# Moving the splits of two weight products in a two-layer MLP kernel: product 2's into a later matmul, product 7's ahead of product 4's

## The chip, the cores and the metric

The kernel runs on one core of one Trainium2 chip. The metric is device time in microseconds (us), the median of several runs. The engines are named as in the profile: PE (matmul) with PEld (its weight loads), DVE (vector), ACT (scalar), POOL (GpSimd) and SP, which here only issues transfers. Transfers are also issued by POOL; all of them are carried out by the DMA engines.

## The reference

```python
def reference(x, w1, w2):          # x 8x1024x1024, w1 1024x4096, w2 4096x1024, f32
    h = x @ w1
    h = 0.5 * h * (1 + np.tanh(np.sqrt(2 / np.pi) * (h + 0.044715 * h ** 3)))
    return (h @ w2).astype(np.float32)
```

## The kernel before

The 8192 rows of x are taken in eight superblocks of 1024 rows. In each, a first matmul makes g = gelu(x w1), and a second one makes g w2. Operands are f16, sums f32. Both matmuls are done by a Strassen scheme: a 2x2 block product takes seven products (numbered 1 to 7) of sums of blocks in place of eight. Products 1, 2 and 3 take plain blocks of the weights, products 4, 5, 6 and 7 take sums of blocks (`W1_SUM`, `W_SUM`). Where the operands of a product are split once more in the same manner, the product itself is seven smaller ones; the code calls these *inner* ones, and a product that is done so is *deep* here (`Inner`, line 1046; its matmuls are line 1118).

The first two superblocks also prepare data for the others. They keep in DRAM the blocks and sums of w1 and w2 (`w1_d`, `w2_d`) and, for each product m of the second matmul, four further sums of quarters of its weights, **the splits of m** (`in_d[m]`). Superblocks 3 to 8 do all seven products of the second matmul deep and load these splits.

- `matmul1` (line 533) is the first matmul of superblocks 1 and 2 (in the code `sb` 0 and 1). It runs over eight pairs j of columns; each pair is seven products of two halves h, with matmuls of 512 columns (line 499). For each pair of superblock 2 it also makes sums of w1 on DVE (`MadeQuad.sum`, `inner_sums`) and stores them from POOL. `half = 3 if j % 2 else 0` says how many of these jobs stand in the middle of a pair, with the rest at its end.
- `matmul2_made` (line 844) is the second matmul of superblocks 1 and 2. Its products run in the order 1, 2, 5, 6, 3, 7, 4, over four row groups q of 128 rows each; a row group is 16 matmuls of 512 columns (line 1160). One product is deep: product 3 in superblock 1, product 4 in superblock 2.
- `FILL[sb]` (line 46) is an order written by hand: after the matmuls of row group q (or deep step n) of product m, the jobs under `mq` are put into DVE's order. `w` makes a quarter of a sum of w2, `p` makes one split of a product (two DVE instructions of 128x1024) and stores it from POOL (512 KB), `a` makes an inner sum of g for the deep product, `g` sums of g, `x`, `q` and `i` sums of the next superblock's x and w1.
- `split_jobs` (line 995) makes a product's four splits: splits 7 and 4 into tiles of the pool `mp` (tile name `mu`, two buffers), splits 5 and 6 into common tiles (pool `up`, tile name `u`, 24 buffers). In superblock 2 product 7's splits all take common ones. The deep product's weights are its own splits (`deep.y = parts[deep.m]`), so their tiles are held until its steps have used them.
- `split_in_m1` (line 1012) can make splits in `matmul1` of superblock 2 from blocks that it loads back from `w2_d`; `SPLIT_IN_M1` (line 39) is empty, so it isn't used.
- `StoredHalf` (line 270) loads half a quad of w1 operands for superblocks 3 to 8: six groups of 512 KB, of which the group `("s1", "s5")` goes into a `mu` tile, the others into `u` tiles. From half 3 on that `mu` tile is filled by POOL (`make`, line 305). `MadeQuad(0, False, True)` loads the first w1 blocks of superblock 2.

Instructions that are pinned (`keep_in_program_order`) keep the program's order on their engine; other transfers are placed by the compiler's scheduler, but each queue carries them out in the order of its list. A tile can be written only when the last user of its buffer is done, and that includes the landing of a store from it. The row `SPq` in the profile is SP's queue.

Of the kernel before, what the change touches and what calls it, by code (L numbers as in the profile page):

```python
# [35 lines left out]
h40 m54 g121' e20 s0 z73 x37 z21 a1 d' e21 m73 m31 h61 q0 u0 m74 p1 g220  # L36
""".split()
BEGIN = {"m37": (0,), "m24": (1,2), "m34": (3, 4)}
SPLIT_IN_M1 = ()


def slots(table):
# [5 lines left out]
    ;20:g50 w50 w51;21:g51 w52;22:w53 g52;23:g53 p14  # L48
    ;50:w60 w61;51:w62 w63;52:g30 g31;53:g32 g33
    ;60:p35 p36;61:p37 a37;62:p34 a36;63:a35  # L50
    ;31:w70;32:a33;33:w71;34:w72;35:w73;36:p25;37:p26
    ;70:p27 p24;71:w40 w41;72:w42 w43;73:x5;40:x7 x6;41:x3 q5;42:q6 q7 q4
    ;43:i2 i7 i3 i1 i5""".replace("\n    ", "")),
    slots("""10:g60 w50;11:g61 w51;12:g62 w52;13:g63 w53
    ;20:g50 p55;21:g51 p56;22:g52 p57;23:g53 p54
    ;50:w60 w61;51:w62 w63;52:g30 g31;53:g32 g33
    ;60:p65 w70;61:p66 w71;62:p67 w72;63:p64 w73
    ;30:w40 w41;31:w42 w43;32:p45 x5;33:p46 x7
    ;70:p47 a47;71:p44 a46;72:a45 p75;73:p76
    ;41:a43;42:p77;43:p74;44:x6;45:x3;46:i2;47:i3""".replace("\n    ", "")),  # L60
)


# [11 lines left out]
def kernel(  # L75
# [457 lines left out]
    def matmul1(xs, sb, quads, start=None):  # L533
# [26 lines left out]
        for j in range(NI // 2):  # L560
            cs = (2 * j, 2 * j + 1)
            end = j == NI // 2 - 1
            source = quads[j // 2]
            if start is not None and j == 0:
                start.pair(gelu)
                ahead(j)
                continue
            jobs = list(ahead(j))
            banks_a = [psum(), psum()]
            a = [temp(), temp()]  # L570
            for h in range(2):
                product(banks_a[h], source, xs, 1, cs[h], True)
                act_copy(a[h], banks_a[h])
            banks_c, p5, t = [], [], [temp(), temp()]

            def five(h):
                if len(p5) == h:
                    banks_c.append(psum())
                    p5.append(temp())
                    product(banks_c[h], source, xs, 5, cs[h], True)  # L580
                    act_copy(p5[h], banks_c[h])

            def six(h):
                product(banks_a[h], source, xs, 6, cs[h], False)
                act_copy(t[h], banks_a[h])

            def seven(h):
                product(banks_a[h], source, xs, 7, cs[h], False)
                tt(p5[h], banks_a[h], p5[h], SUB, True)

            def three(h):
                product(banks_c[h], source, xs, 3, cs[h], False)

            banks_b = [psum(), psum()]
            for h in range(2):
                if late is not None:
                    gelu("12", late[1][h], late[3][h])
                if j == 0:
                    product(banks_b[h], source, xs, 2, cs[h], True)
                if late is not None:  # L600
                    product(late[2][h], late[0], xs, 4, late[1][h], False)
                    gelu("21", late[1][h], late[2][h])
                elif j == 0:
                    five(h)
            for h in range(2 if j else 0):
                product(banks_b[h], source, xs, 2, cs[h], True)
            for h in range(2):
                add(a[h], banks_b[h])
            difference(g, j - 1)
            half = (len(jobs) + 1) // 2  # L610
            if start is not None and j == 1:
                rest = jobs[2:]
                half, jobs = 2, [lambda m=m: quads[0].sum(m, (2, 2), True) for m in (7, 4)] + jobs[:2]
            elif start is not None and j == 2:
                half, jobs = 2, rest
            if sb == 1:
                half = 3 if j % 2 else 0
                if j != 4:
                    jobs += splits
                    splits = []  # L620
            for job in jobs[:half]:
                job()
            if end:
                six(0)
                gelu("11", cs[0], a[0])
                six(1)
                gelu("11", cs[1], a[1])
                for h in range(2):
                    five(h)
                for h in range(2):  # L630
                    seven(h)
                    gelu("22", cs[h], p5[h])
                    three(h)
                for h in range(2):
                    product(banks_a[h], source, xs, 4, cs[h], False)
                    gelu("21", cs[h], banks_a[h])
                for h in range(2):
                    tt(t[h], t[h], banks_c[h], SUB, True)
                    gelu("12", cs[h], t[h])
            else:  # L640
                first = j == 0
                five(0)
                if not first:
                    gelu("11", cs[0], a[0])
                five(1)
                six(0)
                if not first:
                    gelu("11", cs[1], a[1])
                six(1)
                for h in range(2 if first else 0):  # L650
                    gelu("11", cs[h], a[h])
                three(0)
                three(1)
                seven(0)
                seven(1)
                for h in range(2):
                    gelu("22", cs[h], p5[h])
                for h in range(2):
                    tt(t[h], t[h], banks_c[h], SUB, True)
                late = (source, cs, banks_a, t)  # L660
            for job in jobs[half:]:
                job()
            if sb == 1 and j < 2 * len(SPLIT_IN_M1):
                splits = split_in_m1(SPLIT_IN_M1[j // 2], j % 2)
            if sb == 1 and j > 4:
                for q in {5: (0,), 6: (1,), 7: (2, 3)}[j]:
                    nxt["xb"] = x_cast_paced(sb + 1, g["11"][:, 2 * j + 1, :], 2 * q, nxt.get("xb"))
# [176 lines left out]
    def matmul2_made(sb, g, keep_w1, xb):  # L844
# [44 lines left out]
        def rows(t, q):  # L889
# [3 lines left out]
        operands = {1: "11", 2: "12", 4: "22", 7: "21", 5: "11", 3: "12"}  # L893
        parts = {m: {} for m in (1, 2, 3, *SUMS)}
        splits = {
            m: split_jobs(m, lambda m=m: pieces(m), parts[m], () if sb and m == 7 else (7, 4)) for m in parts
        }
        deep = Inner((3, 4)[sb], g[("12", "22")[sb]])
        deep.y = parts[deep.m]

        def run(key):
            for job in FILL[sb].get(key, ()):
# [6 lines left out]
                elif kind == "g":  # L909
                    tt(rows(g["12"], n), rows(g["12"], n), s2[n], SUB, True)  # L910
                elif kind == "w":
                    make(m, n)
                elif kind == "p":
                    splits[m][SUMS.index(n)]()
                elif kind == "a":
                    deep.make(n)
                elif kind == "x":
                    xs.make(m, pin=True)
                elif kind == "q":
                    quad.sum(m, pin=True)  # L920
                elif kind == "i" and sb:
                    xs.make_inner(m)
                elif kind == "i":
                    quad.inner_sums(m)

        into = []
        before_deep = {3: 6, 4: 7}[deep.m]

        def post(m, q, bank):
            if m == before_deep:  # L930
                if q % 2 == 0:
                    into.append(half())
                so_far = into[q // 2][:, q % 2, :]
            if m == before_deep == 6:
                tt(so_far, p5[q], bank, ADD, True)
            elif m in (1, 5, 6):
                t = {1: a, 5: p5, 6: t6}[m]
# [6 lines left out]
            else:  # L944
                t = {2: a, 3: t6, 7: p5}[m][q]
                tt(t, t, bank, ADD, True)
                at[q] = store(sb, {2: "11", 3: "12", 7: "22"}[m], q, t)
            if m == before_deep == 7:
                act_copy(so_far, bank)

        bring("11", pool_copy, False)
# [6 lines left out]
        for m, name, first in (  # L958
            (1, "a", True), (2, "b", True), (5, "c", True), (6, "a", False),
            (3, "c", False), (7, "a", False), (4, "a", False),  # L960
        ):
            if m == deep.m:
                deep.pieces = pieces(m)
                deep.base = into
                deep.rows = lambda r, t: store_rows(sb, {3: "12", 4: "21"}[m], r, t)
                for n in deep.steps(into):
                    if n == 7 and sb == 0:
                        quad = MadeQuad(0, False, True)
                    if n == 1 and sb:
                        quad = StoredHalf(0)  # L970
                    run((m, n))
                continue
            for q in range(NQ):
# [8 lines left out]
                    xs = XOps(x_transpose(xb, load_in_order))  # L982
                if (m, q) == (6, 0):
                    keep("22")
                if (m, q) == (1, NQ - 1) and sb == 0:
                    sums[5] = [unit(2, HALF) for _ in range(NI // QC)]
                    for t in sums[5]:
# [4 lines left out]
                run((m, q))  # L992
        return xs, [quad]

    def split_jobs(m, pieces, t, narrow=(7, 4)):

        def operand(v, h):
            if isinstance(v, int):
# [3 lines left out]

        def make(n):
            u, op, v = W_SUM[n]
            t[n] = (mp.tile([P, NI // 2, OH // 2], DT, name="mu") if n in narrow else unit(NI // 2, OH // 2))
            for h in range(2):
                tt(t[n][:, h * QC:(h + 1) * QC, :], operand(u, h), operand(v, h), op, True)
            nc.gpsimd.dma_start(out=in_d[m][:, SUMS.index(n)], in_=t[n])
# [3 lines left out]
    def split_in_m1(m, h):  # L1012
# [7 lines left out]
        def make(i, n):  # L1020
            u, op, v = W_SUM[n]
            if i % 2 == 0:
                t["two"] = gcp.tile([P, 2, HALF], DT, name="gc")
            t[n] = t["two"][:, i % 2]
            in0, in1 = (
                t[b] if isinstance(b, int) else raw[int(b[0]) - 1][:, int(b[1]) - 1] for b in (u, v)
# [272 lines left out]
```

## Time and profile before

| | |
|---|---|
| median of three runs | 1464.2 us (1462.4, 1464.2, 1464.36) |
| the profiled execution | 1462.14 us |
| its span, first to last instruction | 1460.4 us |
| PE busy / DVE busy / ACT busy / POOL busy | 99% / 84% / 46% / 42% |
| granted TensorE clock | 0.999 |
| second superblock, first matmul | 207.9 to 306.8 us |
| second superblock, second matmul | 306.8 to 401.9 us (product 3 from 362.0, product 7 from 375.9, deep product 4 from 389.6) |
| bytes moved by DMA | 472.73 MB, 324 GB/s over the span |

A line of a timeline gives the start and the length of a group of neighbouring instructions, engine, line, operation, `out<-in` by tile names, the count, and in brackets how long the engine stood idle before and what ended that. A line of waits gives who waited for whom: the sum in us, how often, and the longest. A line of the windows gives, for a stretch of time, each engine's busy us, then the granted clock, the busy share of the DMA engines and the GB/s that they moved.

### The profile page before, as it was taken

Reading aid. Unit: us, or ns where it says so; the run is one execution under the profiler, and the core shown is the slowest. Engines: PE = TensorE matmul, PEld = TensorE weight load, DVE = VectorE, ACT = ScalarE, POOL = GpSimd, SP = SyncE. Lnnn points to the kernel's source line nnn. Section 1 sums busy time; section 2 is a strip of 40 time slices with the busy share of each in tenths; the row PEclk is TensorE's granted clock in tenths of the full one; section 3 lists DMA queues with packets and bytes.
Section 4 is the critical chain, followed back from the end, with each engine's and each line's share of the span. In section 5 each row is a group of like instructions: output and inputs, shape, how many; then the busy total and the mean of one; then the engine's idle time right before and its main releaser. Section 6 shows DMA issues by size and latency. Waiting matters only on the chain.

```text
span 1460.4 us, 28936 instructions
## 1 busy us (share of the span) xinstructions
PE 1446.1 (99%) x10731; PEld 1046.6 (72%) x10731; DVE 1230.3 (84%) x2053; ACT 678.8 (46%) x1402; POOL 620.2 (42%) x630
## 2 busy tenths in 40 slices
PE   8999999999999999999999999999999999999998
PEld 4444644444567888778877788777887778877887
DVE  5657878657888999889998899988998889988887
ACT  5665016631068511784128831388215872068510
POOL 1542222212359411792138821498105961168311
PEclk9999999999999999999999999999999999999999
DMA  9999999797899999999999999999999999996597
GB/s 314 353 349 382 323 319 362 277 281 252 296 353 278 296 351 357 388 254 340 333 382 357 243 373 333 386 322 240 398 335 371 310 263 376 357 386 220 215 370 251
DMA packets 205646, 472.73 MB, mean 324 GB/s; under 512 B 75584, under 2 KB 80704, under 8 KB 204608
## 3 DMA queue, kind: packets, MB, share of 16 engines
q1 hardware_dynamic: 177632, 373.35, 73.8%
q0 software_dynamic: 27872, 97.53, 22.3%
q8 instruction: 84, 1.38, 0.4%
q14 instruction: 58, 0.48, 0.1%
HBM read 370.15 MB, written 115.34 MB: 332 GB/s over the span
## 4 chain that ended last, share of the span: by engine, by line
PE 82%; DMA 11%; issue 2%; POOL 1%; SPq 1%; DVE 1%; ACT 0%; POOLq 0%; DVEq 0%; ACTq 0%
PE ps L1118 35%; PE ps L714 22%; PE ps L499 18%; PE ps L1160 6%; DMA gc<-in_w_dram 5%; DMA u<-in_w_dram 2%; DMA u<-w_d 2%; SPq L164 1%; POOL u L170 1%; PE ps L432 1%; DVE u L140 1%; DMA u<-in_d 1%; DMA w_d<-u 1%; DMA xb<-in_x_dram 1%; DMA out_dram<-tmp 0%
## 5 line engine op out<-in xcount | busy, mean ns | idle before, releaser
L167 ACT COPY tmp<-ps 128x512 f32<-128x512 f32 (+1 forms) x528 | 264.1, 539 | 288.6 <-PE ps L499 178.7
L499 PE MATMUL ps<-u 128*128 128x512 f16 x1472 | 343.5, 379 | 3.1 <-ACT tmp L167 1.8
L1118 PE MATMUL ps<-u,gc 128*128 128x256 f16 x2688 | 301.0, 273 | 0.0
L1118 PEld LDWEIGHTS <-gc 128*128 128x128 f16 x2816 | 275.5, 98 | 32.1 <-DVE u L140 0.3
L842 POOL DMA_DIRECT2D out_dram<-u x74 | 66.9, 943 | 463.9 <-DVE u L140 242.5
L140 DVE TENSOR_TENSOR tmp<-tmp,ps 128x256 f32<-128x256 f32 (+1 forms) x368 | 197.3, 544 | 73.9 <-PE ps L714 29.5
L499 PEld LDWEIGHTS <-u 128*128 128x128 f16 x1472 | 143.9, 98 | 145.4 <-issue 3.9
L714 PEld LDWEIGHTS <-u 128*128 128x128 f16 x2096 | 205.0, 98 | 57.5 <-issue 0.2
L167 ACT COPY u<-ps 128x512 f32<-128x512 f32 (+1 forms) x138 | 80.4, 587 | 352.6 <-PE ps L1118 318.8
L1118 PE MATMUL ps<-u,g 128*128 128x256 f16 x1984 | 226.9, 273 | 0.6 <-DMA u<-w_d 0.6
L1118 PEld LDWEIGHTS <-g 128*128 128x128 f16 x2112 | 206.5, 98 | 25.3 <-DMA u<-w_d 0.9
L140 DVE TENSOR_TENSOR u<-u 128x2048 f16<-128x2048 f16 (+3 forms) x268 | 206.7, 809 | 18.2 <-DMA u<-xb 6.9
L714 PE MATMUL ps<-u 128*128 128x256 f16 x1372 | 221.2, 273 | 0.1
L512 ACT ACTIVATE g<-tmp 128x512 f16<-128x512 f32 x282 | 173.8, 638 | 53.4 <-DVE tmp L140 53.0
L140 DVE TENSOR_TENSOR ps<-tmp,ps 128x256 f32<-128x256 f32 x444 | 181.4, 426 | 19.2 <-PE ps L714 11.9
L140 DVE TENSOR_TENSOR u<-u,ps 128x512 f32<-128x512 f32 x232 | 158.2, 684 | 26.9 <-PE ps L1118 17.7
L512 ACT ACTIVATE g<-ps 128x512 f16<-128x512 f32 x230 | 137.8, 600 | 24.3 <-PE ps L714 14.0
L766 POOL TENSOR_TENSOR tmp<-tmp 128x512 f32<-128x512 f32 x96 | 122.0, 1273 | 41.3 <-DVE tmp L140 30.7
L1160 PE MATMUL ps<-u,g 128*128 128x512 f16 x640 | 138.8, 379 | 0.0
L140 DVE TENSOR_TENSOR tmp<-ps,tmp 128x512 f32<-128x512 f32 x126 | 86.8, 691 | 55.4 <-PE ps L499 42.6
L1160 PEld LDWEIGHTS <-g 128*128 128x128 f16 x640 | 62.6, 98 | 75.3
L140 DVE TENSOR_TENSOR gc<-g,gc 128x2048 f16<-128x2048 f16 x82 | 100.0, 1220 | 1.1 <-PE ps L1118 1.1
(72 smaller groups left out, 1528.7 us busy)
## 6 DMA issues: line engine op xcount, KB each, us to landing
u<-w_d SPq DMA_DIRECT2D x347, 512.0 KB, 10.2
u<-in_d SPq DMA_DIRECT2D x162, 512.0 KB, 10.5
out_dram<-u POOLq DMA_DIRECT2D x74, 512.0 KB, 10.6
gc<-in_w_dram SPq DMA_DIRECT2D x48, 512.0 KB, 6.0
g<-w_d SPq DMA_DIRECT2D x45, 512.0 KB, 14.9
w_d<-u POOLq DMA_DIRECT2D x40, 512.0 KB, 7.6
w_d<-u SPq DMA_DIRECT2D x32, 512.0 KB, 10.2
xb<-in_x_dram POOLq DMA_DIRECT2D x56, 256.0 KB, 7.0
```

Of the source, the lines that this page charges most:

```text
L140: i = nc.vector.tensor_tensor(out=out, in0=in0, in1=in1, op=op)
L164: return tc.keep_in_program_order(nc.sync.dma_start(out=out, in_=in_, **kw))
L167: tc.keep_in_program_order(nc.scalar.copy(out=out, in_=in_))
L170: pool_last[0] = nc.gpsimd.tensor_copy(out=out, in_=in_)
L432: tc.keep_in_program_order(nc.tensor.matmul(bank[:, cols], lhsT=w[:, k, :], rhs=self.xs.blocks[f"{a}{r}"][:, k, cols], start=r == 1 and k ...
L499: tc.keep_in_program_order(nc.tensor.matmul(bank, lhsT=w, rhs=x, start=first and k == 0, stop=k == n - 1, skip_group_check=not first,))
L512: gelu_last[0] = nc.scalar.activation(out=out, in_=src, func=GELU, scale=scale)
L714: tc.keep_in_program_order(nc.tensor.matmul(out, lhsT=w, rhs=x, start=first and k == 0, stop=k == 1, skip_group_check=not first,))
L766: tc.keep_in_program_order(nc.gpsimd.tensor_tensor(out=t, in0=t, in1=temp("p", m), op=ADD))
L842: return nc.gpsimd.dma_start(out=rows, in_=src, **kw)
L1118: tc.keep_in_program_order(nc.tensor.matmul(bank[:, i * OH // 2:(i + 1) * OH // 2], lhsT=t[:, c, i * P:(i + 1) * P], rhs=self.weights(j, c ...
L1160: tc.keep_in_program_order(nc.tensor.matmul(pair(bank), lhsT=a[:, c, :], rhs=chunks(pieces[c // QC])[:, :, c % QC, :], start=(first and c ...
```

## The change

1. Superblock 1, second matmul: the four splits of product 2 (`p25 p26 p27 p24`) leave product 3 and product 7. The quarters `w40` to `w43` spread over that place. The load of superblock 2's first w1 blocks (`MadeQuad(0, False, True)`) is put into the program after the first row group of product 7, no longer after product 3's last step.
2. Superblock 2, first matmul: at the ends of pairs 2 and 3 the blocks of product 2 are loaded back (twice two transfers of 512 KB, into the `gc` pool), and at the ends of pairs 4 and 6 the splits are made from them: in each four DVE instructions of 128x1024 into `mu` tiles, and four stores of 256 KB.
3. Superblock 2, second matmul: product 7's splits are made in product 3's row groups, one by one ahead of `w40` to `w43`, and their splits 7 and 4 go into `mu` tiles. Product 4's splits and the sums `x5`, `x7` follow in product 7's row groups; split 4 of product 4 and the inner sum `a45` come only within deep product 4. All four splits of product 4 take common tiles.
4. The deep product is held in a dict with its own base sums; which products are deep stays the same.

```diff
-SPLIT_IN_M1 = ()
+SPLIT_IN_M1 = {2: 2, 3: 2}
...
-    ;31:w70;32:a33;33:w71;34:w72;35:w73;36:p25;37:p26
-    ;70:p27 p24;71:w40 w41;72:w42 w43;73:x5;40:x7 x6;41:x3 q5;42:q6 q7 q4
+    ;31:w70;32:a33;33:w71;34:w72;35:w73;37:w40
+    ;70:w41;71:w42;72:w43;73:x5;40:x7 x6;41:x3 q5;42:q6 q7 q4
...
-    ;30:w40 w41;31:w42 w43;32:p45 x5;33:p46 x7
-    ;70:p47 a47;71:p44 a46;72:a45 p75;73:p76
-    ;41:a43;42:p77;43:p74;44:x6;45:x3;46:i2;47:i3""".replace("\n    ", "")),
+    ;30:p75 w40;31:p76 w41;32:p77 w42;33:p74 w43
+    ;70:p45 x5;71:p46 a47;72:x7 p47;73:a46
+    ;41:a45;42:p44;43:a43;44:x6;45:x3;46:i2;47:i3""".replace("\n    ", "")),
...
-                if j != 4:
-                    jobs += splits
-                    splits = []
+                if j in (4, 6):
+                    jobs += splits.pop(0)
...
-            if sb == 1 and j < 2 * len(SPLIT_IN_M1):
-                splits = split_in_m1(SPLIT_IN_M1[j // 2], j % 2)
+            if sb == 1 and j in SPLIT_IN_M1:
+                splits.append(split_in_m1(SPLIT_IN_M1[j], len(splits)))
...
-                    if n == 7 and sb == 0:
-                        quad = MadeQuad(0, False, True)
...
+                if (m, q) == (7, 0) and sb == 0:
+                    quad = MadeQuad(0, False, True)
...
-            t[n] = (mp.tile([P, NI // 2, OH // 2], DT, name="mu") if n in narrow else unit(NI // 2, OH // 2))
+            t[n] = (mp.tile([P, NI // 2, OH // 2], DT, name="mu") if n in (7, 4) and m != 4 else unit(NI // 2, OH // 2))
...
-                t["two"] = gcp.tile([P, 2, HALF], DT, name="gc")
+                t["two"] = mp.tile([P, 2, HALF], DT, name="mu")
```

More of the change, by code (lines that the diff above doesn't have):

```diff
@@ L895, in matmul2_made @@
         splits = {
-            m: split_jobs(m, lambda m=m: pieces(m), parts[m], () if sb and m == 7 else (7, 4)) for m in parts
+            m: split_jobs(m, lambda m=m: pieces(m), parts[m]) for m in parts
         }
-        deep = Inner((3, 4)[sb], g[("12", "22")[sb]])
-        deep.y = parts[deep.m]
+        deep = {m: Inner(m, g[operands[m]]) for m in ((3,), (4,))[sb]}
+        for m, d in deep.items():
+            d.base = []
+            d.rows = lambda r, t, o={3: "12", 4: "21"}[m]: store_rows(sb, o, r, t)
+        deep[3 + sb].y = parts[3 + sb]
         def run(key):
@@ L915, in run @@
                 elif kind == "a":
-                    deep.make(n)
+                    deep[m].make(n)
+                elif kind == "l":
+                    deep[m].load((n,))
                 elif kind == "x":
@@ L924, in run @@
                     quad.inner_sums(m)
-        into = []
-        before_deep = {3: 6, 4: 7}[deep.m]
         def post(m, q, bank):
-            if m == before_deep:
+            after = deep.get({6: 3, 7: 4}.get(m))
+            if after:
                 if q % 2 == 0:
-                    into.append(half())
-                so_far = into[q // 2][:, q % 2, :]
-            if m == before_deep == 6:
+                    after.base.append(half())
+                so_far = after.base[q // 2][:, q % 2, :]
+            if after and m == 6:
                 tt(so_far, p5[q], bank, ADD, True)
@@ L947, in post @@
                 at[q] = store(sb, {2: "11", 3: "12", 7: "22"}[m], q, t)
-            if m == before_deep == 7:
+            if after and m == 7:
                 act_copy(so_far, bank)
@@ L961, in matmul2_made @@
         ):
[L962 to L966, printed above, removed]
-                    if n == 7 and sb == 0:
-                        quad = MadeQuad(0, False, True)
-                    if n == 1 and sb:
+            if m in deep:
+                deep[m].pieces = pieces(m)
+                for n in deep[m].steps(deep[m].base):
+                    if (m, n) == (4, 1) and sb:
                         quad = StoredHalf(0)
@@ L993, in matmul2_made, with split_jobs @@
         return xs, [quad]
-    def split_jobs(m, pieces, t, narrow=(7, 4)):
+    def split_jobs(m, pieces, t):
         def operand(v, h):
```

## The prediction

> **What bounds the kernel now.** I read the page first, then PE's waits, then PE's timeline, then, for each wait found, SP's queue and the windows of that stretch.
>
> ```profile
> span 1460.4 us, 28936 instructions
> ...
> PE 1446.1 (99%) x10731; PEld 1046.6 (72%) x10731; DVE 1230.3 (84%) x2053; ACT 678.8 (46%) x1402; POOL 620.2 (42%) x630
> ...
> DMA  9999999797899999999999999999999999996597
> ```
>
> PE is busy for 99% and the DMA engines reach nine tenths in 34 of 40 slices. The change adds or removes no matmul, so it can only win back what PE stands idle. All of PE's waits after the first 28 us:
>
> ```profile
> PE ps L499 <- ACT tmp L167: 1.8, 2, 1.6
> PE ps L499 <- DVE tmp L140: 0.7, 1, 0.7
> PE ps L1118 <- DMA u<-w_d: 0.6, 1, 0.6
> PE ps L499 <- DMA u<-w_d: 0.6, 1, 0.6
> ```
>
> In time, those near the change:
>
> ```profile
> 210.36 10.53 PE L499 MATMUL ps<-u 128*128 128x512 f16 x48 [0.57 <-DMA u<-w_d]
> 221.58 7.93 PE L499 MATMUL ps<-u 128*128 128x512 f16 x36 [0.69 <-DVE tmp L140]
> ...
> 431.63 1.02 PE L499 MATMUL ps<-u 128*128 128x512 f16 x4 [1.59 <-ACT tmp L167]
> ```
>
> The idle time in brackets leaves out the pipelining. From start to start, matmuls of 512 columns follow each other at 0.216 us. Against that PE loses 0.73 at 210.35, 0.85 at 221.58, 0.34 at 229.68, 0.09 and 0.16 at 234.08 and 242.01: **2.17 us at the start of superblock 2**. At 431.63 to 433.64 it loses 1.75 + 0.24 + 0.26: **2.25 us at the start of superblock 3**. The wait at 569.37 (0.81 the same way) lies beyond the change. So the change can win 4.4 us at most; what it may lose has no such bound.
>
> **Part 1: product 2's splits leave superblock 1.** Gone are eight DVE instructions (0.60 each behind one another, by the 128x1024 rows at 162.01, 1.29 for two) and four stores of 512 KB. DVE waits for PE there, so its 5 us are worth nothing. The stores are worth something, for SP's queue runs through that time without a pause:
>
> ```profile
> 149.15 20.39 SPq L164 DMA_DIRECT2D w_d<-u  x5
> 169.77 31.61 SPq L164 DMA_TRANSPOSE u<-xb  x16
> 201.54 36.83 SPq L200 DMA_DIRECT2D u<-w_d  x12
> ```
>
> Sixteen transposing loads of x hold back superblock 2's first w1 loads until 201.54. One by one in SP's rows, the seven from 192.2 take 1.22 to 1.29 each, but the four issued at 181.7, 183.5, 186.1 and 188.8 fill 10.5 us, 5.4 more than four at 1.28. In just this stretch POOL issues product 2's four stores (181.6 to 187.4, the last landed at 194.8) beside 1.5 MB of output. If the extra time goes by bytes, the 2 MB that vanish are 4/7 of it, 3.1 us; the bounds are 0 (output alone holds the transposes up) and 5.4. I take 3.1. What is needed: the wait at 210.35 is for the block landed at 210.31, so 0.8 is enough. That at 221.58 is behind DVE, which works without a real pause from 207.62, when the first block has landed, to 220.9; with the first wait gone too PE would be there 1.58 us earlier, so 1.6 is enough. The smaller ones are followers (that at 229.68 hangs on a store queued behind the same work). So this is a threshold: 2.17 us if the loads come 1.6 earlier. The later place of `MadeQuad` in the program costs nothing: its loads still stand behind the transposes, which cover it by some 15 us. `w43` now ends near 192.7, and product 4 wants it at 196.6.
>
> **Part 2: the same splits in superblock 2's first matmul.** Added: four loads and the eight DVE instructions (2.5 us in pair 4, 2.5 in pair 6), and eight stores of 256 KB. On DVE:
>
> ```profile
> 270.84 2.48 DVE L140 TENSOR_TENSOR u<-u 128x2048 f16<-128x2048 f16 x2
> 273.36 0.69 DVE L140 TENSOR_TENSOR tmp<-tmp,ps 128x512 f32<-128x512 f32 x1
> ```
>
> The new work of pair 4 comes right after the first row. It pushes the addition at 273.36 by 2.4 us; behind it on ACT stand the gelu at 275.55 (which had 1.5 of room) and the copy at 276.08, which PE needs at 278.3 (1.6 of room). So 3.1 us are free and 2.5 are used: no stall, with 0.6 left; what goes over costs PE one for one. By 287 DVE is down to 0.7 late, and then it stands idle for 4.6 us. In pair 6, DVE idles 2.43 us before 297.53 (the row at 297.53 says so), so 2.5 go in for 0.1 at most. Cost taken: 0, bounds 0 and 0.5. The DMA engines: 4 MB at 1.28 us for 512 KB (the spacing of landings between 424.85 and 429.74, when the queue is full) are 10.2 us. Shares in the windows:
>
> ```profile
> 257.00:269.00 12.00, 12.00 (x58) 5.40 (x56) 7.19 (x15) 7.34 (x15) 1.35 (x2) 1.00 0.58 222
> 269.00:281.00 12.00, 12.00 (x57) 5.45 (x56) 10.62 (x15) 7.34 (x15) 4.17 (x8) 1.00 0.71 236
> ```
>
> There 8.5 us are free (0.42 and 0.29 of 12), and 1.3 in the 12 before. The rest falls into 281 to 306, where w2's loads have landed by 285.7 for a use at 306.8. Cost 0.
>
> The Trainium skill (DMA: Bandwidth & Descriptors, "Measured (HBM→SBUF, 128 partitions, SWDGE, issued from GpSimd)") says that transfers should be batched to 1 MiB or more, and its section "Anatomy of one DMA" gives about 2.0 us fixed plus bytes at 436 GB/s. Added up one after another, the four loads and eight stores would by that take some 34 us (estimate from that page). The trace shows 1.28 us a transfer of 512 KB where several are under way, so by this row the fixed part overlaps.
>
> **Part 3: product 7's splits first.** The wait at 431.63 goes back to a transfer. The chain of waits has POOL's `make` of half 3 at 428.59; it reads a group of w1 whose transfer was issued at 414.89 and by the semaphore's events landed at 428.46, though its `mu` buffer had been free since 416.8. In the next pair POOL is 2.7 us behind the pair's first matmul on `mu`; the same here would be 425.4. So **3.2 us earlier** clears the wait. Why it is late:
>
> ```profile
> 398.56 3.81 SPq L286 DMA_DIRECT2D mu<-w_d  x2
> 402.47 37.34 SPq L286 DMA_DIRECT2D u<-w_d  x24
> ```
>
> SP's waits from 372 to 432, and the window of the deep product:
>
> ```profile
> SPq L286 <- DMA in_d<-mu: 13.6, 1, 13.6
> SPq L286 <- PE ps L1118: 7.5, 1, 7.5
> ```
>
> ```profile
> 390.00:402.00 12.00, 12.00 (x112) 10.73 (x110) 11.96 (x18) 0.59 (x1) 2.40 (x5) 1.00 0.78 287
> ```
>
> SP's queue stands at the first `mu` transfer from 377.2 to 398.56 and at the second from 398.9 to 402.06, because product 4's splits 7 and 4 hold both `mu` buffers until deep steps 5 and 7 are done. Seven transfers wait behind them while the DMA engines idle 2.6 us (0.22 of 12); from 402.5 they are full. After the change the `mu` buffers hold product 7's splits, made near 374 and 378 and stored by about 385, so both transfers go out before 390. Common buffers: four of w2's block 12 come free when product 7 ends (387 to 390) and not after its splits (394.7 to 397.1); product 4's hold theirs until 395 to 402. By my count of the tiles in program order the first loads of half 1 find buffers at 391.1, 391.6, 395.0, 396.8 and 398.5. Product 7's four stores (389.7 to 397.4) move to 366 to 378, where the DMA share is 0.46: 4 x 1.28 = 5.1 us less in the full stretch. Together 7.7; less 1.3 for split 4 of product 4, which is now stored near 395, 6.4 us. Bounds: 2.6 (only the idle time is used) and 7.7. I take 6.4, twice the need: **2.25 us gained**.
>
> What it moves on DVE costs nothing: each row group of products 3 and 7 gets at most 3.1 us of work against 3.45 of PE. In the deep product the slots are the same, with other work in them: `a46` ends at 391.7 (wanted 393.3), `a45` at 393.4 (395.0), split 4 of product 4 at 395.2 (400.3), `a43` at 396.9 (398.5). Cover 1.6 each; past that PE waits one for one.
>
> **Sum.** 2.17 + 2.25 - 0.1 = 4.3 of the profiled execution's 1462.14 (span 1460.4 and 1.7 around it), so 1457.8 there. That execution lies 2.1 below the median of the runs; from the median, 1464.2 - 4.2 = **1460.0**.
>
> **Rivals.**
> - *One of the two starts is mended, not both* (transposes held up by the output stores alone, or half 3 still late by other transfers ahead of it): 2.2 gained, 1462.0. For it: both are thresholds. Chance 0.24, the better half of it for part 3.
> - *Nothing moves*: the queue fills with the next transfers and the same ones land last: 1464. Against it: bytes are taken out of full stretches and put into 0.46 and 0.58. Chance 0.08.
> - *Slower: DVE stands still at pair 4's split.* The reloads aren't pinned. SP's list has a gap between 253.9 and 270.7; if they stand before it, they have landed by 262. If they come behind the four w2 loads issued from 270.7 to 277.6 (the last landed at 285.7), DVE waits from 273.3 to 286, 12.7 us, and with 2.5 of work less 3.1 of room PE loses 12: 1476. It decides at a landing after 273.9. Chance 0.08.
> - *Slower: every transfer costs its own time.* The shortest time from issue to landing among the `in_d` stores from 362 to 402 is 2.9 us. Twelve such, not overlapping, are 34.8 with 9.8 free; w2's first blocks would land 25 late, at 310.7 against 306.8, and without any gain that is 1468. Chance 0.03. The fixed cost on the page of the Trainium skill named above would do just this.
>
> **Chances.** Forecast 0.57, the rivals 0.24, 0.08, 0.08, 0.03. A difference under 0.2% (2.9 us) is about what a measurement here can't tell from none. The forecast passes it by 1.3 us, about six times in seven, one start alone one time in five: faster 0.55, same 0.33, slower 0.12. Range: from both starts won against the fastest run (1462.1 - 4.4 = 1457.7) to nothing won and a little noise (1464.8); the slower cases, 0.11, are left out.
>
> **What would show it.** Transposes from 181 on at about 1.3 us, the first w1 loads near 198, PE without a wait at 210 and 221. Both `mu<-w_d` transfers issued before 390, the `u<-w_d` ones from about 391, POOL's first `make` near 425. In pair 4 DVE's four 128x1024 rows without idle time ahead of them. I am wrong if PE waits for DVE at 278, or if the first `u<-w_d` load still leaves after 402.

## The result, and the profile after

The changed kernel takes 1473.43 us (median of 22 runs, 1462.86 to 1478.89), the kernel before, measured beside it, 1462.67 (22 runs, 1460.72 to 1466.01): ratio 1.006, 95% interval 1.0042 to 1.0078. It is slower by 9 us by the ratio (6 to 11 by its interval) and by 11 by the medians, where 4 less were forecast, and its times lie 16 apart where those of before lie 5 apart. The profiled execution took 1475.4, its span 1473.6.

PE's matmuls follow each other at a fixed pace. Time above that pace, from start to start in the trace, by stage of the kernel before, us:

| stage of before | before | after |
|---|---|---|
| superblock 2, first matmul (208 to 306.8) | 2.1 | 3.8 |
| superblock 2, second matmul (306.8 to 402) | 0.1 | 3.9 |
| superblock 3, first matmul and half of the second (402 to 543) | 3.3 | 10.3 |

PE's timeline of the changed kernel; the bracket is the idle time ahead and what ended it:

```profile
231.54 2.75 PE L499 MATMUL ps<-u 128*128 128x512 f16 x12 [3.47 <-ACT tmp L167]
...
397.29 8.79 PE L1118 MATMUL ps<-u,gc 128*128 128x256 f16 x64 [2.14 <-DVE u L140]
...
412.58 0.61 PE L713 MATMUL ps<-u 128*128 128x256 f16 x4 [2.12 <-DMA u<-w_d]
414.25 2.27 PE L499 MATMUL ps<-u 128*128 128x512 f16 x5 [1.06 <-DMA u<-w_d]
```

The waits of before at 210, 221 and 431.6 are gone; these have come in their place. They have two beginnings. (One more of 2.2, for `u<-in_d`, stands at 509.9; with the stretch at half clock behind it, it is about 4 of the 10.3. No other trace has it, and its cause was not followed.)

**First beginning: where the reloads went.** SP's queue in the changed kernel:

```profile
169.50 28.11 SPq L164 DMA_TRANSPOSE u<-xb  x16
197.72 2.58 SPq L200 DMA_DIRECT2D u<-w_d  x4
200.34 3.43 SPq L1018 DMA_DIRECT2D gc<-w_d  x4
203.87 4.64 SPq L200 DMA_DIRECT2D u<-w_d  x4
```

The first w1 loads leave at 197.7 (201.5 before), as forecast. But line 1018, the reloads, stands right behind them, ahead of the w1 loads of the next quad (203.87). Those land at 218.6 to 229.6 by the semaphore events, against 211.5 to 219.0 before. DVE sums them, and stands still:

```profile
222.17 1.23 DVE L140 TENSOR_TENSOR u<-u 128x2048 f16<-128x2048 f16 x1 [1.03 <-DMA u<-w_d]
225.83 1.23 DVE L140 TENSOR_TENSOR u<-u 128x2048 f16<-128x2048 f16 x1 [2.44 <-DMA u<-w_d]
228.20 1.55 DVE L140 TENSOR_TENSOR u<-u 128x512 f16<-128x512 f16 x4 [1.15 <-DMA w_d<-u]
229.67 1.28 DVE L140 TENSOR_TENSOR tmp<-tmp,ps 128x512 f32<-128x512 f32 x2
```

The addition at 229.67 releases ACT, and ACT releases PE at 231.54.

**Second beginning: the transposes of x for superblock 3.** SP's queue, first of the kernel before, then of the changed one:

```profile
312.87 31.27 SPq L164 DMA_TRANSPOSE u<-xb  x16
```

```profile
315.09 63.29 SPq L164 DMA_TRANSPOSE u<-xb  x16
393.04 4.68 SPq L286 DMA_DIRECT2D mu<-w_d  x2
397.80 2.27 SPq L286 DMA_DIRECT2D u<-w_d  x4
```

The 16 transposes take twice as long from first to last. Two windows of the changed kernel (the last two columns are the DMA engines' busy share and GB/s; the share adds up the packets' times of all queues, so it can pass 1):

```profile
348.00:362.00 14.00, 14.00 (x67) 6.34 (x65) 9.98 (x13) 2.35 (x4) 4.07 (x7) 1.00 1.28 143
...
376.00:390.00 14.00, 14.00 (x67) 6.34 (x66) 10.74 (x15) 1.17 (x2) 4.64 (x8) 1.00 1.26 169
```

The engines are busier than ever (1.28, 1.26) and move less than half of what they move elsewhere (408 at 1.04 from 208 to 220). Stores and transposes slow each other down (e9 below tests this). A store of a split lands late, so its `mu` buffer comes free late: DVE waits 2.8 for one at 381.45, and 2.1 for a transpose at 392.48, which is PE's wait at 397.29. The `mu<-w_d` transfers leave at 393.04, where before 390 was forecast; half 0's other loads stand behind them in SP's list (in the kernel before they stood ahead and left at 372.2). Hence 412.58 and 414.25.

### The profile page after: what moved, and what is told of

The parts are those of the page before. It is cut to its first block, busy times and chain, and to the rows that moved or that the text cites. A ratio compares the mean times of both kernels' runs of the same rounds, so it can differ in the third digit from the quotient of the medians.

```text
span 1473.6 us, 28952 instructions
## 1 busy us (share of the span) xinstructions
PE 1451.5 (98%) x10731; PEld 1048.5 (71%) x10731; DVE 1231.9 (84%) x2053; ACT 679.0 (46%) x1402; POOL 624.5 (42%) x634
## 4 chain that ended last, share of the span: by engine, by line
PE 70%; DMA 5%; DVE 1%; issue 0%; POOL 0%; SPq 0%; ACT 0%; DVEq 0%; POOLq 0%
PE ps L1118 35%; PE ps L713 22%; PE ps L499 13%; DMA in_d<-mu 2%; DMA u<-w_d 1%; DMA w_d<-u 1%; DVE u L140 1%; DMA u<-in_d 0%; DVE ps L140 0%; DVE tmp L140 0%; DVE mu L140 0%; SPq L286 0%; POOL tmp L765 0%; ACT tmp L167 0%; POOL mu L317 0%
## 5 line engine op out<-in xcount | busy, mean ns | idle before, releaser
L1118 PE MATMUL ps<-u,gc 128*128 128x256 f16 x2704 | 306.0, 274 | 4.3 <-DMA u<-in_d 2.2
```

The lines of the kernel that those rows point to most:

```text
L1118: tc.keep_in_program_order(nc.tensor.matmul(bank[:, i * OH // 2:(i + 1) * OH // 2], lhsT=t[:, c, i * P:(i + 1) * P], rhs=self.weights(j, c ...
```

## The experiments

Medians and ratios to the kernel before, measured beside each; the last column is the lowest and the highest time.

| kernel | median us | ratio (95%) | from - to |
|---|---|---|---|
| e1: part 3 alone | 1460.98 | 0.9997 (0.9985 - 1.0009) | 1459.1 - 1466.3 |
| e2: parts 1 and 2 alone | 1468.82 | 1.0056 (1.0032 - 1.0081) | 1463.9 - 1483.4 |
| e3: reloads later | 1463.68 | 1.0013 (0.9993 - 1.0033) | 1457.5 - 1474.1 |
| e4: product 2's splits left out | 1458.42 | 0.9970 (0.9960 - 0.9981) | 1456.5 - 1459.5 |
| e6: e3 without the splits' stores | 1458.72 | 0.9982 (0.9970 - 0.9993) | 1456.9 - 1466.2 |
| e7: e4 with 2 MB of idle loads | 1458.34 | 0.9973 (0.9964 - 0.9981) | 1456.1 - 1460.4 |
| e8: splits in the second matmul | 1458.66 | 0.9974 (0.9964 - 0.9983) | 1456.1 - 1461.3 |
| e9: e4 with 2 MB of idle stores | 1473.49 | 1.0067 (1.0049 - 1.0085) | 1468.9 - 1474.7 |
| e10: transposes later | 1464.84 | 1.0016 (1.0005 - 1.0027) | 1462.1 - 1468.6 |
| e11: part 1 alone, splits as in e8 | 1458.15 | 0.9967 (0.9955 - 0.9978) | 1457.0 - 1460.4 |
| e12: e3 and e10 together | 1459.68 | 0.9983 (0.9972 - 0.9995) | 1457.2 - 1462.0 |

**Which part loses.** e1 is the kernel before with the new `FILL[1]` and tiles, e2 the changed kernel with the old ones.

```diff
 # e1, from the kernel before
-    ;30:w40 w41;31:w42 w43;32:p45 x5;33:p46 x7
-    ;70:p47 a47;71:p44 a46;72:a45 p75;73:p76
-    ;41:a43;42:p77;43:p74;44:x6;45:x3;46:i2;47:i3
+    ;30:p75 w40;31:p76 w41;32:p77 w42;33:p74 w43
+    ;70:p45 x5;71:p46 a47;72:x7 p47;73:a46
+    ;41:a45;42:p44;43:a43;44:x6;45:x3;46:i2;47:i3
```

> The kernel before with part 3 alone: in superblock 2's second matmul product 7's splits stand in product 3's row groups and take the mu tiles, product 4's follow and take common tiles; product 2's splits stay in superblock 1. Three theories of the 10.8 us that the change lost (medians). T1, the reloads' place in SP's list (issued 200.3 to 203.2, ahead of quad 1's w1 loads) starts a chain of lateness that reaches the deep product: then this kernel has no such chain, the product 7 stores have landed by 385, the first mu load of superblock 3 leaves before 385 and half 0's loads behind it before 390, the wait at 431.6 is gone, and the time is 0 to 3 us under the kernel before (ratio 0.998 to 1.000). T2, part 3 itself loses: SP's list has both mu loads ahead of half 0's five loads, these leave after 395, PE waits near 412, and the product 7 stores hold up the transposes of x; 3 to 8 us over the kernel before (1.002 to 1.0055). T3, the added transfers as such (2 MB read back, eight stores of 256 KB): this kernel has none of them, 0 to 3 us under.

> The kernel before with parts 1 and 2 alone: product 2's splits leave superblock 1 and are made from reloaded blocks in superblock 2's first matmul; product 4's and product 7's splits keep the order and the tiles of the kernel before. T1 (place of the reloads): the waits at 210 and 221 go (-2.2), the wait of 3.6 at 231.5 comes, the later half of superblock 2's w1 sums is stored some 5 us later and the second batch of transposes of x is held up as in the changed kernel; the stages from 200 to 400 lose 3 to 6 us, with the wait of the kernel before at 431.6 still there: 2 to 8 us over (1.0015 to 1.0055). T2 (part 3 is what loses): -2.2 from part 1 and +3.6 at 231.5, nothing behind that: 0 to 1.5 over (1.000 to 1.001). T3 (added transfers as such): like T1.

e1 is the same as before within its interval, e2 loses as much as the whole change: T2 falls. In e1 the queue moves as the prediction had it:

```profile
378.46 6.88 SPq L286 DMA_DIRECT2D mu<-w_d  x2
385.45 14.08 SPq L286 DMA_DIRECT2D u<-w_d  x10
```

Both `mu` transfers leave before 390, half 0's loads behind them early enough, POOL's first `make` of half 3 runs at 423.31 (428.59 before), and PE's wait at 431.6 is gone.

**The place of the reloads, and the splits themselves.** e3 puts the reloads behind quad 2's w1 loads; e4 leaves product 2's splits out.

```diff
 # e3, from the changed kernel
-                    nc.sync.dma_start(out=halves(self.raw[b]), in_=w1_at(q, term.get(b, b)))
+                    self.loaded = nc.sync.dma_start(out=halves(self.raw[b]), in_=w1_at(q, term.get(b, b)))
...
-                splits.append(split_in_m1(SPLIT_IN_M1[j], len(splits)))
+                with tc.issue_after(quads[-1].loaded.ins):
+                    splits.append(split_in_m1(SPLIT_IN_M1[j], len(splits)))
 # e4, from the changed kernel
-SPLIT_IN_M1 = {2: 2, 3: 2}
+SPLIT_IN_M1 = {}
```

> The changed kernel, with the four reloads placed in SP's list behind the w1 loads of quad 2 of superblock 2's first matmul, no longer ahead of quad 1's; the split work on DVE stands where it stood. T1 (place of the reloads): quad 1's loads leave near 200 and have landed by 220, no wait at 231.5, everything behind is 3 to 5 us earlier, half 0's loads leave before 392; the time falls to that of the kernel before or under it (0.997 to 1.000). T2 (part 3 loses): only the 3.6 at 231.5 goes, the waits at 397, 412 and 414 stay: 1.003 to 1.005. T3 (added transfers as such): the reloads now meet the w2 loads issued from 270; DVE waits at pair 4's split or the w2 loads land later, and the loss stays: 1.004 or more.

> The changed kernel with parts 1 and 3, but product 2's splits are not made at all: no reloads, no work for them on DVE, no stores of them; superblocks 3 to 8 load product 1's splits in their place, so this part of the computation is changed. T1 (place of the reloads) and T3 (the added transfers as such): both foresee the full gain that was forecast, 3 to 5 us under the kernel before (0.9965 to 0.998). T2 (part 3 loses): the waits at 412 and 414 stay, 1 to 6 us over (1.0005 to 1.004). Beside the kernel with the later reloads this tells T1 from T3.

e4 gives the forecast gain, so T2 falls again. e3 wins 10 of the 15 us between the changed kernel and e4, as T1 has it, but its median is 5 above e4 and over T1's range, and its times lie 17 apart: something is left that T1 doesn't name.

**What is left: one kernel, two executions.**

> The kernel with the later reloads once more, for the trace of another execution: its 12 times lay between 1457.5 and 1474.1, and the profiled one was 1458.2. Theory: what is left of the loss sits where the transposes of x for superblock 3 (first issue 311.2) meet the last w2 loads; in the profiled execution these left at 296.8 to 309.8, against 291.4 to 298.9 in the kernel without product 2's splits. In an execution over 1465 the 16 transposes then take 45 us or more from first to last issue (34.3 in the first trace), and PE waits between 380 and 420; in one under 1461 they take about 34. Rival: the executions differ elsewhere (the loading stretch, the clock, the end), with the transposes at 34 in a slow one too.

The second trace of e3 took 1473.98, the first 1458.16. From 208 to 306 PE loses at most 0.3 in either. Windows of the first, then of the second:

```profile
320.00:334.00 14.00, 14.00 (x66) 6.37 (x65) 10.47 (x14) 0.00 (x0) 3.90 (x8) 1.00 1.16 221
...
348.00:362.00 14.00, 14.00 (x67) 6.36 (x65) 6.08 (x8) 2.35 (x4) 3.52 (x6) 1.00 0.77 271
...
390.00:402.00 12.00, 12.00 (x103) 9.79 (x101) 11.93 (x19) 0.84 (x2) 1.27 (x2) 1.00 1.05 405
```

```profile
320.00:334.00 14.00, 14.00 (x67) 6.34 (x66) 11.02 (x15) 0.00 (x0) 3.78 (x7) 1.00 1.26 145
...
348.00:362.00 14.00, 14.00 (x66) 6.33 (x65) 5.52 (x7) 2.35 (x4) 3.53 (x6) 1.00 1.21 183
...
390.00:402.00 12.00, 7.27 (x41) 5.15 (x39) 9.52 (x12) 0.58 (x1) 3.76 (x7) 0.72 0.99 364
```

The same transfers are asked for, but from 320 to 334 they go at 221 GB/s in the one and at 145 in the other, and PE stands only in the last window. The DMA issues from 320 to 334 (KB each, median us to landing), first and second execution:

```profile
out_dram<-tmp POOLq DMA_DIRECT2D x4, 256.0 KB, 7.0
...
u<-xb SPq DMA_TRANSPOSE x6, 8.9
```

```profile
out_dram<-tmp POOLq DMA_DIRECT2D x4, 256.0 KB, 15.2
...
u<-xb SPq DMA_TRANSPOSE x5, 17.8
```

Both kinds take twice as long. First to last transpose: 34 us against 68. The theory held, its rival didn't.

**Loads or stores beside the transposes.** e6 is e3 without the eight stores. e7 and e9 add to e4 2 MB that nobody waits for: as loads ahead of the transposes, or as stores beside them.

```diff
 # e7, from e4
             bring("22", None, False)
+            for k in range(4):
+                load_in_order(mp.tile([P, 2, HALF], DT, name="mu"), w2_at(k, 2))
 # e9, from e4
-                nc.gpsimd.dma_start(out=w2_at(q, m)[:, :n], in_=sums[m][q][:, :n])
+                done = nc.gpsimd.dma_start(out=w2_at(q, m)[:, :n], in_=sums[m][q][:, :n])
+                if m == 5:
+                    with tc.issue_after(done.ins):
+                        nc.gpsimd.dma_start(
+                            out=in_d[2][:, q].rearrange("p c n -> p (c n)"),
+                            in_=raw["21"][q].rearrange("p c n -> p (c n)"),
+                        )
```

> The kernel with the later reloads, without the eight stores of product 2's splits (2 MB); reloads and DVE work stay; superblocks 3 to 8 load product 1's splits in their place, so that part of the computation is changed. It stands between the kernel with later reloads (1463.7 median, 16.6 wide) and the one without product 2's splits (1458.4, 3 wide). Theory A, the stores are what is left of the loss (they go ahead of w1's last sums on POOL's queue, so buffers come free later and the w2 loads meet the transposes): 1458 to 1460, less than 5 wide. Theory B, the reloads and DVE's work: 1462 to 1464 and over 10 wide.

> The kernel without product 2's splits, with four loads of 512 KB that nobody reads on SP's queue, behind the w2 loads of block 22 and right ahead of the transposes of x (they leave near 299, into mu tiles that are free there). Product 2's splits stay left out, so that part of the computation is changed. Nothing waits for these loads and no buffer comes free later through them. Theory, the transposes suffer when loads are still under way as they start: first to last transpose takes over 45 us in place of 30.5, PE waits between 380 and 420, and the times are 3 to 12 us over the 1458.4 of the kernel without the loads, widely spread. Rival, lateness alone does it (late stores, late buffers): 1458 to 1460, the transposes at 30 to 35 us.

> The kernel without product 2's splits, with four stores of 512 KB that nobody reads on POOL's queue, one behind each store of product 5's weights (309 to 320), so that they are under way as the transposes of x begin (311). Product 2's splits stay left out, so that part of the computation is changed. They hold up nothing but the last reuse of product 2's blocks near 362. Theory, stores under way beside the transposes make both slow (in the second trace of the kernel with later reloads, 256-byte packets took 72 to 109 ns from 320 to 332 where they took 18 to 58 in the first, and the 16 transposes 68 us): here the transposes take over 45 us in most executions and the times are 1462 to 1474, widely spread. Rival, stores do harm only through the buffers that they hold (lateness): 1458 to 1460 and the transposes near 31 us.

e7 costs nothing: the loads put the transposes off to 321.31, and these run in 23.11 us. That loads ahead of them do the harm falls; loads beside them were not tried. e9's median is 15 us over e4's, its fastest run 9 over e4's slowest. SP's queue in e4, then SP's queue and PE in e9:

```profile
311.12 30.45 SPq L164 DMA_TRANSPOSE u<-xb  x16
```

```profile
310.75 72.42 SPq L164 DMA_TRANSPOSE u<-xb  x16
```

```profile
404.43 9.13 PE L1124 MATMUL ps<-u,gc 128*128 128x256 f16 x64 [12.95 <-DVE u L140]
```

By SP's waits no transpose and no load waits for these stores, yet 30.5 us become 72.4, and what DVE wants of x at 387 lands at 399.5. So stores beside the transposes are enough. The added ones have all landed by 333.2; the transposes stay slow to the end, with only the kernel's own stores beside them. e6 agrees, less sharply: without the splits' stores 11 of 12 runs are under 1462, but they lie 9 apart where under 5 was expected.

**Transposes later, and the splits elsewhere.**

```diff
 # e10, from the changed kernel
-                for q in {5: (0,), 6: (1,), 7: (2, 3)}[j]:
+                for q in {5: (0,), 6: (1,), 7: ()}[j]:
...
+                if (m, q) == (2, 1) and sb:
+                    for r in (4, 6):
+                        x_cast_paced(sb + 1, a[1], r, xb)
 # e8, from the changed kernel
-SPLIT_IN_M1 = {2: 2, 3: 2}
+SPLIT_IN_M1 = {}
-    ;60:p65 w70;61:p66 w71;62:p67 w72;63:p64 w73
+    ;60:p65 w70 p25;61:p66 w71 p26;62:p67 w72 p27;63:p64 w73 p24
```

In e8 all splits of product 2 take common tiles. e11 is e8 with the old `FILL[1]` but for this row, and the old tiles of products 4 and 7.

> The changed kernel, with the last four copies of x rows to DRAM made wait for product 2's second row group, so that the transposes of x, which read them, begin near 335 and no longer at 315; reloads and splits as in the changed kernel. Theory, most of the loss behind 306 comes from transposes beginning among the last w2 loads and the stores that queued up behind these: the transposes then take 25 to 35 us, the waits at 397 to 415 are gone, and what is left is the wait of 3.6 at 231.5 against the gains of 4.4: 1461 to 1464 (0.9995 to 1.001), under 8 wide. Rival, the stores of product 5's splits and sums disturb them there as well, or x's sums on DVE come too late: 1470 or more.

> Parts 1 and 3 as in the changed kernel, but product 2's splits are made in superblock 2's second matmul, one behind each row group of product 6 (348 to 362), from the blocks of product 2 that lie in the buffers there, into common tiles: no reloads, and four stores of 512 KB after the transposes of x. DVE is busy 6.4 of 14 us there without them and gets 5 more; the DMA engines are busy 0.66 and 0.55 from 348 to 376. Theory, only the place of the work lost the time: 1458 to 1460 (0.997 to 0.9985), nearly as the kernel without these splits, and the spread is small. Rival, 2 MB of stores cost wherever they stand in this stretch, and four more common tiles are missing for the loads of superblock 3: 1462 to 1466.

> Part 1 alone: product 2's splits leave superblock 1 and are made behind product 6's row groups in superblock 2's second matmul from the blocks that lie there; product 4's and 7's splits keep the order and tiles of the kernel before. If part 1 is worth the forecast 2.2: 1460 to 1461 (0.998 to 0.999), without waits of PE at 210, 221 and 229 and with the one at 431.6. If part 1 only works together with part 3: 1462 to 1464.

> The changed kernel once more, for the trace of another execution. Its 22 times lie between 1462.9 and 1478.9. Theory: every execution has the wait of some 3.6 at 231.5 (the reloads' place); whether it ends near 1463 or near 1475 is decided from 315 on by the transposes: over 60 us from first to last in an execution over 1468, under 40 in one under 1465. Rival: the wait at 231.5 itself varies by that much.

> The changed kernel with both edits: the reloads behind quad 2's w1 loads, and the last four copies of x to DRAM behind product 2's second row group, so that the transposes begin near 340. All of product 2's reloads, splits and stores stay in superblock 2's first matmul. Theory, the loss of part 2 is these two places and nothing else: 1457.5 to 1460 (0.9965 to 0.9985), under 6 wide, the transposes in about 31 us, no wait at 231.5. Rival, the added transfers cost something by themselves: 1461 to 1464. Rival, transposes are disturbed in this place as well in some executions: a spread over 8, as with the later reloads alone (16.6).

In e10 the transposes run from 343.35 in 31.25 us, and behind 306 PE loses only 0.9 more than in e4. What stays is the reloads' wait:

```profile
232.98 7.32 PE L499 MATMUL ps<-u 128*128 128x512 f16 x27 [5.07 <-ACT tmp L167]
```

It came to 1464.8, a little above what I had expected, since the wait was 5.1 and not 3.5 and a stretch at half clock followed it. `after_again` fell at 1476.0, with the 3.5 at 231.66 and 64.96 us of transposes, as an execution over 1468 was expected to; no trace of a changed kernel near 1463 was caught. e12 has both edits and all of part 2's transfers: 1459.7, within 5 us, the transposes in 28.3. By the ratios it is 1 to 2 above e8 and e11, with intervals that touch.

e8 and e11 are faster than both kernels: the splits are made where DVE is idle and after the transposes, from blocks that lie in the buffers, without reloads. e8's window there:

```profile
348.00:362.00 14.00, 14.00 (x67) 6.32 (x65) 9.82 (x14) 2.35 (x4) 5.19 (x10) 1.00 0.84 322
```

## Why the prediction was wrong

**Part 1 was right, and its size too small.** Transposes from 181 on take 1.15 to 2.24 us, mostly 1.26, the first w1 loads leave at 197.7, and PE has no wait at 210 or 221. In e11 the stage from 208 to 306.8 goes from 2.1 above pace to -0.1: the 2.17 of the forecast. The wait at 431.6 goes too, but for 0.5 behind it (402 to 543: 3.3 to 1.7); I had given it to part 3 alone. It doesn't always go with part 1: in e2's trace, where PE comes 18 us late, it stands at 449.24 with 1.39. Together e11 is 3 to 7 us under the kernel before.

**Part 2: "Cost 0" is the step that failed, in two of its terms.** What I looked at most closely held: DVE makes pair 4's splits without idle time ahead of them (275.09 to 277.70), and PE has no wait at 278. Nor did my other sign of being wrong show: the first `u<-w_d` load leaves at 397.80, ahead of 402.

- *The reloads' DMA, which I had put into free time from 245 on.* They aren't pinned, I had said so, and asked only what happens if they come too late; an earlier place was harmless to me ("they have landed by 262"). The scheduler put them at 200.34, into a queue that was full (DMA share 0.97 from 200 to 208, 1.04 from 208 to 220). e10 less e8 prices it by medians: 6.2 us, of which 5.1 is the wait and the rest the half clock behind it.
- *The stores' DMA, which was to fit because 8.5 us were free.* I added bytes at 1.28 us for 512 KB, as if what runs beside them had no part in it. The place also shifts others. On POOL's queue in the kernel before, then in the changed one:

```profile
276.94 0.68 POOL L245 DMA_DIRECT2D w_d<-u  x1 [2.65 <-DVE u L140]
278.08 0.68 POOL L245 DMA_DIRECT2D w_d<-u  x1 [0.46 <-DVE u L140]
279.54 0.68 POOL L258 DMA_DIRECT2D w_d<-u  x1 [0.79 <-DVE u L140]
280.11 0.30 POOL L479 COPY pace<-g 128x2 f16<-128x2 f16 x1
```

```profile
276.07 2.47 POOL L1029 DMA_DIRECT2D in_d<-mu  x4
280.60 1.22 POOL L479 COPY pace<-g 128x2 f16<-128x2 f16 x1 [2.06 <-ACT g L512]
...
282.27 1.44 POOL L245 DMA_DIRECT2D w_d<-u  x2
```

  Three of the w1 sums' stores now stand behind the `pace` copy, which waits for ACT; before, they left ahead of it. Their buffers come free later, w2's last loads leave at 301 to 313.6 instead of 292.7 to 300.6, and the stores behind these meet the transposes of x. e9 shows that stores there do the harm, e10 that taking the transposes away mends it: 8.6 us by medians. e12 shows that the two places are nearly the whole loss: 6.2 and 8.6 are 14.8 of the 15.0 between the changed kernel and e4. The division is rough: e3, which mends the first place alone, wins 9.8.

**Part 3: right alone, worth nothing beside part 1.** e1 shows each step (the `mu` transfers before 390, POOL's `make` early, the wait gone, 2.2 less from 402 to 543 in its trace, that of its fastest run), though its runs are only 0.9 under, -2.2 to +1.3. The need of "3.2 us earlier" was too large. In e11, with the old order and the first `mu` transfer still at 396.63, half 3's group landed 3.6 earlier, at 424.82, 1.7 of it against PE's own progress (PE is 1.93 ahead there). POOL's `make` still starts 0.13 behind that landing, as in the kernel before; the bracket names only the last of its waits:

```profile
424.95 1.15 POOL L317 TENSOR_TENSOR mu<-u 128x512 f16<-128x512 f16 x1 [4.18 <-DVE ps L140]
```

These 1.7 took away 1.75 of PE's 2.25. Where the group gained them is not settled. So one wait was to be won, and in these traces either part wins it. In the changed kernel part 3 adds a hazard: the `mu` transfers stand ahead of half 0's loads, which costs nothing while they leave at 378 and 3.2 us of PE when they leave at 393.

**The rivals.** The slower case that I priced at 1476 came near the time by luck, for it came about another way: DVE did not wait for the reloads; the w1 loads behind the reloads did. "Every transfer costs its own time" is refuted: e12 has all twelve added transfers and is under the kernel before. The Trainium skill (DMA: Bandwidth & Descriptors, "Anatomy of one DMA") gives each transfer a fixed cost of about 2 us; that such costs add up for transfers under way together is not what e12 shows. The 0.12 for slower lacked the case that happened, an unpinned transfer that comes too early.

**What stays open.** Why e3 falls to one side or the other at 316 to 320 with the same list of transfers isn't settled; from 308 to 316 its two traces move 359 and 366 GB/s. No run put loads beside the transposes, so whether it must be stores is open. Which of the stores weigh most was not separated, nor whether e12's last 1 to 2 us are real.

## What to carry to other kernels

A moved transfer has two ends: ask what it delays if it comes too early, not only who waits if it is late, and pin it where both are fine. A free DMA share was no room here for stores beside DMA transposes; look for a window without them, or move the transposes. A wait can be won only once, so forecast gains should not be added without asking whether one part alone would win both.

## What the runs showed of the hardware

**Transposes and stores.** The 8192 packets of 256 bytes of the 16 transposes took 22 and 21 ns in the mean in e8 and e11, but 75 in e9 and 67 in the second trace of e3. The median is 18 in all four, so a part of the packets takes very long. The four output stores issued from 318 to 340 landed after 2.3 to 4.7 us in e8 and e11, after 13.4 to 17.1 in the other two. The Trainium skill (DMA: Bandwidth & Descriptors, "Rules for kernel authors") says that a transpose next to ordinary DMAs needs nothing; nothing here speaks against that for the data, but in time it cost e9 15 us.

**Half clock after short waits.** The clock records fall to 0.5 in steps of 3.413 us on a fixed grid: in the second trace of e3 the window from 390 to 402 has 0.72. Over fifteen traces, from 150 to 700 us, each grid step at full clock with PE idle for 2.12 us or more was followed by one at 0.5, and none with 1.94 or less; four steps already at 0.5 were followed by another with 0.9 to 1.45 idle. So a wait costs its length and up to 1.7 more for each such step, by where it falls on the grid. The Trainium skill (TensorE: Matmul & The Clock Gate, "Part 1: The HAM clock gate") has the same 3413 ns, free-running, but an idle window as the condition; here about 60% of one was enough.
